# Early part of a decoder block: groups of 1, 1, 2, 2, 2, 4, 4 chunks of w_in, and the norm of x by tokens

## The chip, the cores and the metric

The kernel runs on one core of a Trainium2 chip. The metric is the time of one launch in microseconds (us) as the device reports it; lower is better. One execution of each kernel is taken by the hardware profiler, and its span runs from the first to the last instruction. The engines are TensorE (PE, with its weight loads as PEld), VectorE (DVE), ScalarE (ACT), GpSimd (POOL) and SyncE (SP), which issues most transfers.

## The reference

A decoder block on one sequence of 256 tokens, width 2048, all in fp32. Only its beginning matters here:

```python
c_act = jax.nn.silu(c)
mod = (c_act @ w_ada[l] + b_ada[l])[:, None, :]
sh1, sc1, gt1, sh2, sc2, gt2 = jnp.split(mod, 6, axis=-1)
h = rms_norm(x, g_pre_mix[l]) * (1.0 + sc1) + sh1
z = h @ w_in[l]
...
# two attention branches on z, gates, w_o; then the same with sh2, sc2 and a ConvFFN (w_up, w_down)
```

w_ada is 2048 x 12288 and w_in 2048 x 8000, so both are read once from HBM and used for one vector and 256 tokens.

## The kernel before

Channels lie on the partitions: x is held as xT, 16 chunks of 128 channels by 256 tokens. A product of fp32 numbers is made of three products of rounded ones. Each weight tile of 128 x 1024 (512 KB) is loaded into a buffer raw, ACT casts it to whi (L116), DVE makes wlo as the difference (L117), and PE multiplies whi by h, whi by the low part of h, and wlo by h (mm3, L129 to L131; mm3t, L144 to L146, with the sides swapped). Of raw, whi and wlo there are five buffers each (NW1).

The early part computes a first share of z: 39 blocks of 128 columns of w_in, which end in 20 pairs (tiles of 128 x 512 in SBUF). It runs over groups of chunks of the inner dimension (KGS = 2, 2, 2, 2, 4, 4), so that it can begin before all of w_ada's two first parts (sh1 and sc1) is there. For each group, early_gen makes h of the group's chunks: xT times rstd (L264), the adaLN product of c with the group's columns of w_ada (ada_gen), its result turned onto the partitions by a small matmul (L270), the columns s1 and sh1 (L275 to L277), x times s1 plus sh1 (L282), and the split of h into high and low (split_pair, L158 and L159). Then early_z runs the 39 blocks over the group's chunks; in the first group an ACT copy makes the pairs (L368), in later ones DVE adds to them (L375), or ACT copies and POOL adds for every third pair (L372, L373). The products of one pair end in one of three PSUM banks ("mm").

ada_gen loads tiles of 512 KB into raw2 (four buffers, L102); for the first group every other one goes to raw instead (L95, spread). A chunk takes four such tiles. In each, PE multiplies cpad (silu of c, one column of 32) by the four column groups of the tile (L234). From the fourth group on every second tile is multiplied on DVE instead (SHARE, L240 and L242) and summed by four matmuls (L247).

Ahead of all this x's norm: ACT squares xT by two chunks (L211, two buffers), PE sums over the partitions with a matrix of ones (L213), ACT takes the root (L215) and DVE the reciprocal (L216), all with tokens in the free dimension.

A generator (bg) interleaves the next group's early_gen with the present group's early_z in the program; then a scheduler, which models the engines' times, fixes the order of the instructions on each engine. Each engine works through its own order and waits for semaphores; SP does the same with the transfers. Behind the early part, the matmul that begins the band bias (L328) and the latents' norms (lat) stand in the last group's hooks.

Of the kernel before, what the change touches and what calls it, by code (L numbers as in the profile page):

```python
# [20 lines left out]
NF = DFF // P  # L21
EPS = 1e-6
NEG = -1e30
KGS = [2, 2, 2, 2, 4, 4]
SHARE = [99, 99, 99, 2, 2, 2]
NEARLY = 8
LATS = (3, 4, 5, 6, 7, 8, 9)
HOOKS = (3, 9, 15)
# [10 lines left out]
WT = 1024  # L39
# [4 lines left out]
def block_kernel(ctx: ExitStack, tc: tile.TileContext, a, out: bass.AP):  # L44
    nc = tc.nc
    pe, act, dve, pool = nc.tensor, nc.scalar, nc.vector, nc.gpsimd
    PS = bass.MemoryType.PSUM

    const = ctx.enter_context(tc.tile_pool(name="const", bufs=1))
    dram = ctx.enter_context(tc.tile_pool(name="dram", bufs=1, space=bass.MemoryType.DRAM))  # L50
    hp_ctx = ExitStack()
    hp = hp_ctx.enter_context(tc.tile_pool(name="hp", bufs=8, side="right"))
# [5 lines left out]
    def bank(tag):  # L58
        return psp.tile([P, 512], F32, tag=tag, bufs=PSN[tag], name="bk_" + tag)
# [88 lines left out]
    def turn_pe(o, x):  # L148

        pe.transpose(o, x, ident)  # L150

    split_ins = []

    def split_pair(src, pl, tag, bufs, eng=dve):

        hl = pl.tile([P, 2, 2, T], F32R, tag=tag, bufs=bufs // 2, name=tag)
        src = src.rearrange("p (j t) -> p j t", j=2)
        i0 = act.copy(hl[:, :, 0], src)  # L158
        i1 = eng.tensor_tensor(hl[:, :, 1], src, hl[:, :, 0].bitcast(F32), op=ALU.subtract)  # L159
        split_ins[:] = [i0, i1]  # L160
        return [(hl[:, j, 0], hl[:, j, 1], hl[:, j].rearrange("p a t -> p (a t)")) for j in range(2)]


    blk_ctx = ExitStack()
# [11 lines left out]
    xT = xp.tile([P, KC, T], F32, name="xT")  # L176
# [28 lines left out]
    dve.tensor_copy(cpad[:, :, 0:1], csil.rearrange("p (k o) -> p k o", o=1))  # L205


    ps_ss = bank("tp")
    for k in range(0, KC, 2):
        sq = xp.tile([P, 512], F32, tag="sq", bufs=2, name="sq").rearrange("p (a b) -> p a b", a=2)  # L210
        act.activation(sq, xT[:, k:k + 2, :], AF.Square)  # L211
        for i in range(2):
            pe.matmul(ps_ss[:, :T], ones, sq[:, i, :], start=(k + i == 0), stop=(k + i == KC - 1))  # L213
    rstd = xp.tile([P, T], F32, name="rstd")
    act.activation(rstd, ps_ss[:, :T], AF.Sqrt, scale=1.0 / D, bias=epst)  # L215
    dve.reciprocal(rstd, rstd)  # L216
# [36 lines left out]
    s1 = const.tile([P, KC], F32, name="s1")  # L253
    sh1 = const.tile([P, KC], F32, name="sh1")
    hs = [None] * KC

    def early_gen(kg, k0, s):

        w = s * 64
        with ExitStack() as order:  # L260
            if kg:
                order.enter_context(tc.issue_after(split_ins[1].ins))
            for k in range(k0, k0 + s):
                dve.tensor_tensor(xT[:, k, :], xT[:, k, :], rstd, op=ALU.mult)  # L264
        yield from ada_gen(a["w_ada1"][kg], w, rows, 0, "sc", SHARE[kg], kg == 0)

        nb = w // P
        ps = bank("tp")
        for b in range(nb):
            pe.matmul(ps[:, 4 * b:4 * b + 4], rows[:, b * P:(b + 1) * P], ident[:, 0:P:32], start=True, stop=True)  # L270

        pv = ps[:, :4 * nb].rearrange("p (b g) -> p g b", g=4)
        bs = bada[:, KC + k0:KC + k0 + s].rearrange("p (g b) -> p g b", g=2)
# [12 lines left out]
    sh2 = const.tile([P, KC], F32, name="sh2")

# [51 lines left out]
    def early_z(kg, hooks):  # L339
        s, k0 = KGS[kg], k0s[kg]  # L340
        nblk = 2048 // (s * P)
        order = []
        for i in range(NPAIR):
            order += [("kr", 6)] if i == 6 else [("vs", 7), ("vs2", 7)] if i == 7 else [(0, i), (1, i)]
        src = a["w_in1"][kg]
        b = None
        for off in range(0, len(order), nblk):
            n = min(nblk, len(order) - off)
            w = n * P * s
            wt = Weights(src[:, off * P * s:off * P * s + w], w, WT if n == nblk else n * P * (s // 2))  # L350
            for u in range(n):
                what, i = order[off + u]
                if what in (0, "kr", "vs"):
                    b = bank("mm")
                if what == "vs":
                    for half in range(2):
                        for kk in range(s):
                            mm3t(b[:, half * T:half * T + T], wt.cut(kk * n * P + u * P, 2 * P), hs[k0 + kk], half,
                                 kk == 0, kk == s - 1)
                elif what != "vs2":  # L360
                    c0 = T if what == 1 else 0
                    for kk in range(s):
                        mm3(b[:, c0:c0 + T], wt.cut(kk * n * P + u * P), hs[k0 + kk], kk == 0, kk == s - 1)
                if what in (1, "kr", "vs2"):
                    wd = T if i == 6 else 2 * T
                    if kg == 0:
                        pairs[i] = blkp.tile([P, 512], F32, tag="blk", name="pair")
                        act.copy(pairs[i][:, :wd], b[:, :wd])  # L368
                    elif i % PADD == 1:
                        pl = xp if kg < len(KGS) - 1 else at  # L370
                        part = pl.tile([P, 512], F32, tag="sq" if pl is xp else "tmp", bufs=2, name="part")
                        act.copy(part[:, :wd], b[:, :wd])  # L372
                        pool.tensor_tensor(pairs[i][:, :wd], pairs[i][:, :wd], part[:, :wd], op=ALU.add)  # L373
                    else:
# [543 lines left out]
```

## Time and profile before

| | us |
|---|---|
| median of 3 runs | 1507.36 |
| lowest and highest | 1503.29, 1513.49 |
| profiled execution | 1507.02 |
| its span | 1505.2 |
| PE busy in it | 1455.3 (97%) |
| DVE busy in it | 1080.4 (72%) |
| ACT busy in it | 781.5 (52%) |

The span is what the trace shows from the first to the last instruction; 1.8 us of the execution lie around it. A busy share is an average over the whole span: the early part is its first sixth, and its own bound is read from its own stretches.

### The profile page before, as it was taken

Reading aid. Unit: us, or ns where it says so; the run is one execution under the profiler, and the core shown is the slowest. Engines: PE = TensorE matmul, PEld = TensorE weight load, DVE = VectorE, ACT = ScalarE, POOL = GpSimd, SP = SyncE. Lnnn points to the kernel's source line nnn. Section 1 sums busy time; section 2 is a strip of 40 time slices with the busy share of each in tenths; the row PEclk is TensorE's granted clock in tenths of the full one; section 3 lists DMA queues with packets and bytes.
Section 4 is the critical chain, followed back from the end, with each engine's and each line's share of the span. In section 5 each row is a group of like instructions: output and inputs, shape, how many; then the busy total and the mean of one; then the engine's idle time right before and its main releaser. Section 6 shows DMA issues by size and latency. Waiting matters only on the chain.

```text
span 1505.2 us, 24750 instructions
## 1 busy us (share of the span) xinstructions
PE 1455.3 (97%) x9506; PEld 1280.5 (85%) x9506; DVE 1080.4 (72%) x1472; ACT 781.5 (52%) x1253; POOL 294.9 (20%) x207
## 2 busy tenths in 40 slices
PE   7999999789999899999899999999999999999997
PEld 6988899789898899978688888888888888888886
DVE  3579868988787969777788878877767776444443
ACT  4534435545645555766465545655555555434442
POOL 0034315832524535420000000000000000000000
PEclk9999999999999999999999999999999999999999
DMA  9889868588587858658667778765555557555552
GB/s 373 320 309 325 307 234 263 178 266 289 187 295 238 291 186 268 228 201 336 245 207 270 254 258 263 247 209 186 191 188 192 187 193 243 191 196 190 190 193 99
DMA packets 101525, 356.96 MB, mean 237 GB/s; under 512 B 11760, under 2 KB 12208, under 8 KB 100896
## 3 DMA queue, kind: packets, MB, share of 16 engines
q1 hardware_dynamic: 99936, 350.82, 67.9%
q0 software_dynamic: 1472, 4.58, 1.2%
q8 instruction: 74, 1.21, 0.3%
q14 instruction: 43, 0.35, 0.1%
HBM read 351.11 MB, written 4.24 MB: 236 GB/s over the span
## 4 chain that ended last, share of the span: by engine, by line
PE 72%; DMA 12%; DVE 9%; issue 3%; ACT 2%; POOL 1%; DVEq 0%; SPq 0%; ACTq 0%; POOLq 0%
PE bk_mm L136 10%; PE bk_sc L136 7%; DMA raw<-in_w_ada_dram 6%; PE bk_mm L129 6%; PE bk_mm L131 6%; PE bk_mm L130 6%; PE bk_mm L138 5%; PE bk_mm L144 4%; PE bk_mm L146 4%; PE bk_mm L145 4%; DVE wlo L117 3%; PE bk_sc L145 3%; PE bk_sc L144 3%; PE bk_sc L146 3%; PE bk_sc L138 3%
## 5 line engine op out<-in xcount | busy, mean ns | idle before, releaser
L117 DVE TENSOR_TENSOR wlo<-raw,whi 128x1024 fp32r<-128x1024 f32 (+3 forms) x472 | 589.5, 1257 | 278.0 <-ACT whi L116 276.8
L116 ACT CAST whi<-raw 128x1024 fp32r<-128x1024 f32 (+3 forms) x472 | 478.3, 1021 | 487.7 <-DMA raw<-in_w_up_dram 74.6
L129 PE MATMUL bk_mm<-h,whi 128*128 128x256 f32 x976 | 282.6, 290 | 0.1
L130 PE MATMUL bk_mm<-h,whi 128*128 128x256 f32 x976 | 277.8, 285 | 0.0
L131 PE MATMUL bk_mm<-h,wlo 128*128 128x256 f32 x976 | 277.3, 285 | 0.5 <-DVE wlo L117 0.5
L136 PE MATMUL bk_mm<-h,whi 128*128 128x512 f32 x848 | 266.6, 396 | 0.0
L242 DVE SCALAR_TENSOR_TENSOR acc<-raw,csil,acc 128x1024 f32<-128x1024 f32 (+1 forms) x141 | 190.6, 1352 | 45.1 <-DMA raw<-in_w_ada_dram 44.3
L129 PEld LDWEIGHTS bk_mm<-h,whi 128*128 128x128 f32 x976 | 187.7, 193 | 13.6 <-issue 9.1
L138 PEld LDWEIGHTS bk_mm<-h,wlo 128*128 128x128 f32 x848 | 158.9, 188 | 41.1 <-DVE wlo L117 3.9
L130 PEld LDWEIGHTS bk_mm<-h,whi 128*128 128x128 f32 x976 | 187.9, 193 | 0.8 <-issue 0.8
L131 PEld LDWEIGHTS bk_mm<-h,wlo 128*128 128x128 f32 x976 | 187.6, 193 | 0.9 <-DVE wlo L117 0.7
L136 PE MATMUL bk_sc<-h,whi 128*128 128x512 f32 x560 | 177.0, 398 | 0.0
L138 PE MATMUL bk_mm<-h,wlo 128*128 128x256 f32 x848 | 167.5, 279 | 1.5 <-DVE wlo L117 1.5
L136 PEld LDWEIGHTS bk_mm<-h,whi 128*128 128x128 f32 x848 | 129.2, 189 | 0.5 <-issue 0.4
L138 PEld LDWEIGHTS bk_sc<-h,wlo 128*128 128x128 f32 x560 | 105.3, 189 | 27.5 <-DVE wlo L117 2.8
L762 POOL TENSOR_TENSOR sa<-sa,u 128x512 f32<-128x512 f32 x22 | 33.7, 1531 | 467.8 <-DVE u L756 387.0
L138 PE MATMUL bk_sc<-h,wlo 128*128 128x256 f32 x560 | 110.8, 279 | 1.7 <-DVE wlo L117 1.7
L373 POOL TENSOR_TENSOR pair<-pair,part 128x512 f32<-128x512 f32 x35 | 63.4, 1812 | 192.3 <-ACT part L372 192.2
L136 PEld LDWEIGHTS bk_sc<-h,whi 128*128 128x128 f32 x560 | 85.8, 190 | 0.4 <-ACT whi L116 0.4
L144 PE MATMUL bk_sc<-whi,g 128*128 128x512 f32 x176 | 68.7, 390 | 0.0
L144 PE MATMUL bk_mm<-whi,g 128*128 128x512 f32 x176 | 68.7, 390 | 0.0
L145 PE MATMUL bk_mm<-wlo,g 128*128 128x512 f32 x176 | 68.5, 389 | 0.0
(205 smaller groups left out, 2317.6 us busy)
## 6 DMA issues: line engine op xcount, KB each, us to landing
raw<-in_w_ada_dram SPq DMA_DIRECT2D x192, 512.0 KB, 5.1
raw<-in_w_up_dram SPq DMA_DIRECT2D x176, 512.0 KB, 4.6
raw<-in_w_in_dram SPq DMA_DIRECT2D x116, 512.0 KB, 5.2
raw<-in_w_down_dram SPq DMA_DIRECT2D x88, 512.0 KB, 4.5
raw<-in_w_o_dram SPq DMA_DIRECT2D x32, 512.0 KB, 5.6
raw<-in_w_uqn_dram SPq DMA_DIRECT2D x16, 384.0 KB, 4.0
bias<-trow POOLq DMA_DIRECT2D x16, 256.0 KB, 4.8
raw<-in_w_ukv_dram SPq DMA_DIRECT2D x16, 256.0 KB, 3.5
```

Source lines behind the costliest of these rows:

```text
L116: act.copy(hi[:, :n], raw[:, :n])
L117: dve.tensor_tensor(lo[:, :n], raw[:, :n], hi[:, :n].bitcast(F32), op=ALU.subtract)
L129: pe.matmul(o, wh, xh, start=start, stop=False)
L130: pe.matmul(o, wh, xl, start=False, stop=False)
L131: pe.matmul(o, wl, xh, start=False, stop=stop)
L136: pe.matmul(o, w[0], x[2], start=start and i == 0, stop=False)
L138: pe.matmul(o[:, :T], w[1], x[0], start=False, stop=stop and i == 1)
L144: pe.matmul(o, ch, wh, start=start, stop=False)
L145: pe.matmul(o, ch, wl, start=False, stop=False)
L146: pe.matmul(o, cl, wh, start=False, stop=stop)
L242: dve.scalar_tensor_tensor(acc[:, :w], r, csil[:, j:j + 1], acc[:, :w], op0=ALU.mult, op1=ALU.add)
L373: pool.tensor_tensor(pairs[i][:, :wd], pairs[i][:, :wd], part[:, :wd], op=ALU.add)
```

## The change

The groups become 1, 1, 2, 2, 2, 4, 4 chunks; the products on DVE begin with the fifth group, which is the same chunk as before. A group of one chunk has 64 columns in each of the four column groups of the adaLN product, so a small matmul has 64 columns instead of 128, and two matmuls (L287) turn the result. split_pair can split a single chunk; two single chunks share one buffer. The first adaLN product no longer spreads its tiles over two pools. The norm's sums are taken with the squares as the stationary operand and one column of ones as the moving one, so that the tokens end on the partitions: 32 matmuls (L223) into two banks, a root of two columns (L226), a reciprocal of 128 x 2, and two transposes that bring the result back to the free dimension (L230, in turn_pe), copied by ACT (L232). A root of a constant (L216) is taken ahead of the squares.

```diff
-KGS = [2, 2, 2, 2, 4, 4]
-SHARE = [99, 99, 99, 2, 2, 2]
+KGS = [1, 1, 2, 2, 2, 4, 4]
+SHARE = [99, 99, 99, 99, 2, 2, 2]
...
-    ps_ss = bank("tp")
+    warm = const.tile([P, 1], F32, name="warm")
+    act.activation(warm, epst, AF.Sqrt, scale=0.0, bias=epst)
+    ps_ss = [bank("tp"), bank("o")]
     for k in range(0, KC, 2):
         sq = xp.tile([P, 512], F32, tag="sq", bufs=2, name="sq").rearrange("p (a b) -> p a b", a=2)
         act.activation(sq, xT[:, k:k + 2, :], AF.Square)
         for i in range(2):
-            pe.matmul(ps_ss[:, :T], ones, sq[:, i, :], start=(k + i == 0), stop=(k + i == KC - 1))
+            for t in range(2):
+                pe.matmul(ps_ss[t][:, 0:1], sq[:, i, t * P:t * P + P], ones[:, 0:1], start=(k + i == 0), stop=(k + i == KC - 1))
+    rt = const.tile([P, 2], F32, name="rt")
+    for t in range(2):
+        act.activation(rt[:, t:t + 1], ps_ss[t][:, 0:1], AF.Sqrt, scale=1.0 / D, bias=epst)
+    dve.reciprocal(rt, rt)
+    ps_r = bank("tp")
+    for t in range(2):
+        turn_pe(ps_r[:, t * P:t * P + P], rt[:, t:t + 1].broadcast_to([P, P]))
     rstd = xp.tile([P, T], F32, name="rstd")
-    act.activation(rstd, ps_ss[:, :T], AF.Sqrt, scale=1.0 / D, bias=epst)
-    dve.reciprocal(rstd, rstd)
+    act.copy(rstd, ps_r[:, :T])
...
-        yield from ada_gen(a["w_ada1"][kg], w, rows, 0, "sc", SHARE[kg], kg == 0)
+        yield from ada_gen(a["w_ada1"][kg], w, rows, 0, "sc", SHARE[kg])
...
+        if s == 1:
+            for u in range(2):
+                pe.matmul(ps[64 * u:64 * u + 64, 0:2], rows[:, 0:64], ident[:, 32 * u:P:64], start=True, stop=True)
+            nb, ng = 1, 2
...
-            hs[k:k + 2] = split_pair(xT[:, k:k + 2, :].rearrange("p a b -> p (a b)"), hp, "h", 16)
+            hs[k:k + len(ks)] = split_pair(xT[:, k:k + len(ks), :].rearrange("p a b -> p (a b)"), hp, "h", 16, n=len(ks),
+                                           room=hroom)
...
-            wt = Weights(src[:, off * P * s:off * P * s + w], w, WT if n == nblk else n * P * (s // 2))
+            wt = Weights(src[:, off * P * s:off * P * s + w], w, WT if n == nblk or s == 1 else n * P * (s // 2))
```

The scheduler lays the early part out anew. On SP, at the start of the program, before (w_ada1_0 and w_in1_0 are the first group's tiles, w_ada1_1 the second group's adaLN tiles):

```order
L178 DMA xT_80<-in_xT_dram 128x1024 x4
L102 DMA raw2_155<-in_w_ada1_0_dram 128x1024
L95 DMA raw_165<-in_w_ada1_0_dram 128x1024
L102 DMA raw2_175<-in_w_ada1_0_dram 128x1024
L95 DMA raw_185<-in_w_ada1_0_dram 128x1024
L102 DMA raw2_195<-in_w_ada1_0_dram 128x1024
L95 DMA raw_205<-in_w_ada1_0_dram 128x1024
L102 DMA raw2_215<-in_w_ada1_0_dram 128x1024
L95 DMA raw_225<-in_w_ada1_0_dram 128x1024
L95 DMA raw_246<-in_w_in1_0_dram 128x1024
L102 DMA raw2_255<-in_w_ada1_1_dram 128x1024
L95 DMA raw_265<-in_w_in1_0_dram 128x1024
```

and now, from the last but one adaLN tile of the first group on (x's four and two more stand ahead):

```order
L102 DMA raw2_215<-in_w_ada1_0_dram 128x1024
L102 DMA raw2_233<-in_w_ada1_0_dram 128x1024
L95 DMA raw_262<-in_w_in1_0_dram 128x1024
L95 DMA raw_288<-in_w_in1_0_dram 128x1024
L95 DMA raw_385<-in_w_in1_0_dram 128x1024
L95 DMA raw_409<-in_w_in1_0_dram 128x1024
L95 DMA raw_505<-in_w_in1_0_dram 128x896
L102 DMA raw2_270<-in_w_ada1_1_dram 128x1024
L102 DMA raw2_294<-in_w_ada1_1_dram 128x1024
L102 DMA raw2_391<-in_w_ada1_1_dram 128x1024
L102 DMA raw2_415<-in_w_ada1_1_dram 128x1024
```

The first group's w_in tiles, which alternated with the second group's adaLN tiles, now all stand ahead of them. On PE, around the first product on w_in (L129), before:

```order
L234 MATMUL bk_sc_154<-raw_225,cpad_105 32x128 x8
L270 MATMUL bk_tp_236<-c_ident_85,rows_144 128x4
L234 MATMUL bk_sc_254<-raw2_255,cpad_105 32x128 x8
L129 MATMUL bk_mm_281<-h_243,whi_248 128x256
L129 MATMUL bk_mm_296<-h_243,whi_248 128x256
```

and now:

```order
L150 MATMUL bk_tp_164<-c_ident_85,rt_160 128x128 x2
L250 MATMUL bk_sc_178<-raw2_233,cpad_105 32x64 x6
L250 MATMUL bk_sc_269<-raw2_270,cpad_105 32x64 x16
L250 MATMUL bk_sc_269<-raw2_294,cpad_105 32x64 x3
L287 MATMUL bk_tp_252<-c_ident_85,rows_169 64x2 x2
L250 MATMUL bk_sc_269<-raw2_294,cpad_105 32x64 x13
L250 MATMUL bk_sc_269<-raw2_391,cpad_105 32x64 x16
L250 MATMUL bk_sc_269<-raw2_415,cpad_105 32x64 x2
L129 MATMUL bk_mm_312<-h_259,whi_264 128x256
L129 MATMUL bk_mm_321<-h_259,whi_264 128x256
```

Fifty of the 64 small matmuls of the second group's adaLN product now stand ahead of the first product on w_in, where eight of 64 stood. On ACT, from the last squares to the first h, before:

```order
L211 ACTIVATE sq_137<-xT_80 128x512
L215 ACT_TABLE_LOAD
L215 ACTIVATE rstd_141<-bk_tp_108,epst_89 128x256
L249 COPY rows_144<-bk_sc_154 128x128
L116 CAST whi_248<-raw_246 128x1024
L158 CAST h_243<-xT_80 128x2x256
```

and now:

```order
L220 ACTIVATE sq_148<-xT_80 128x512
L116 CAST whi_264<-raw_262 128x1024
L220 ACTIVATE sq_154<-xT_80 128x512
L116 CAST whi_290<-raw_288 128x1024
L116 CAST whi_387<-raw_385 128x1024
L116 CAST whi_411<-raw_409 128x1024
L226 ACTIVATE rt_160<-bk_tp_110,epst_89 128x1
L226 ACTIVATE rt_160<-bk_o_111,epst_89 128x1
L116 CAST whi_507<-raw_505 128x896
L232 COPY rstd_167<-bk_tp_164 128x256
L265 COPY rows_169<-bk_sc_178 128x64
L165 CAST h_259<-xT_80 128x256
```

The five casts of the first group's w_in tiles, one of which stood ahead of the first h, now all do, four of them ahead of the root of the norm.

## Rows read from the trace of the kernel before

**Rows 1.** The page's busy time of each engine (share of the span, instructions), and the chain that ended last, by engine.

```profile
PE 1455.3 (97%) x9506; PEld 1280.5 (85%) x9506; DVE 1080.4 (72%) x1472; ACT 781.5 (52%) x1253; POOL 294.9 (20%) x207
...
PE 72%; DMA 12%; DVE 9%; issue 3%; ACT 2%; POOL 1%; DVEq 0%; SPq 0%; ACTq 0%; POOLq 0%
```

**Rows 2.** The table by stretches: us, then busy time and instructions of PE, PEld, DVE, ACT and POOL, the granted clock of PE, the busy share of the DMA engines, GB/s.

```profile
0.00:10.00 10.00, 3.92 (x10) 3.21 (x11) 1.02 (x4) 3.35 (x6) 2.13 (x9) 1.00 0.79 277
10.00:20.00 10.00, 9.34 (x136) 6.64 (x134) 1.30 (x1) 4.83 (x7) 0.00 (x0) 1.00 1.02 409
...
30.00:40.00 10.00, 10.00 (x115) 9.01 (x114) 4.60 (x4) 7.21 (x11) 0.00 (x0) 1.00 1.03 407
...
200.00:220.00 20.00, 20.00 (x178) 18.74 (x177) 13.82 (x21) 6.86 (x11) 3.32 (x2) 1.00 0.59 203
...
260.00:280.00 20.00, 19.12 (x150) 18.21 (x149) 20.00 (x15) 14.12 (x18) 19.62 (x10) 1.00 0.64 198
280.00:300.00 20.00, 13.99 (x96) 13.37 (x96) 16.41 (x15) 8.16 (x13) 16.40 (x13) 0.83 0.52 164
```

**Rows 3.** The same table by 2 us around the first product on w_in; the granted clock is the last but two.

```profile
23.00:25.00 2.00, 1.63 (x19) 1.25 (x20) 1.68 (x2) 0.66 (x2) 0.00 (x0) 0.63 1.03 412
25.00:27.00 2.00, 2.00 (x12) 2.00 (x11) 1.96 (x4) 0.67 (x1) 0.00 (x0) 0.51 1.03 410
27.00:29.00 2.00, 2.00 (x28) 1.67 (x28) 0.73 (x1) 1.05 (x1) 0.00 (x0) 1.00 1.03 410
```

**Rows 4.** The timeline of PE up to the first product on w_in: start, us, engine, line, operation, out<-in, count of records (an fp32 matmul has two), and in brackets the idle time before and what ended it.

```profile
6.08 6.61 PE L213 MATMUL bk_tp<-sq,ones 128*128 128x256 f32 x20 [6.08 <-ACT sq L211]
...
20.06 0.65 PE L234 MATMUL bk_sc<-raw,cpad 128*32 128x128 f32 x16 [0.62 <-DMA raw<-in_w_ada_dram]
21.09 0.39 PE L270 MATMUL bk_tp<-c_ident,rows 128*128 128x4 f32 x2 [0.38 <-ACT rows L249]
23.37 0.98 PE L234 MATMUL bk_sc<-raw,cpad 128*32 128x128 f32 x16 [1.90 <-DMA raw<-in_w_ada_dram]
24.27 1.01 PE L129 MATMUL bk_mm<-h,whi 128*128 128x256 f32 x3
```

**Rows 5.** The timeline of ACT, same columns.

```profile
5.30 1.15 ACT L211 ACTIVATE sq<-xT 128x512 f32<-128x512 f32 x2 [2.67 <-DMA xT<-in_xT_dram]
...
16.90 1.28 ACT L215 ACT_TABLE_LOAD   x1 [1.85 <-PE bk_tp L213]
18.19 0.47 ACT L215 ACTIVATE rstd<-bk_tp,epst 128x256 f32<-128x256 f32 x1
20.77 0.27 ACT L249 COPY rows<-bk_sc 128x128 f32<-128x128 f32 x1 [2.10 <-PE bk_sc L234]
21.32 1.05 ACT L116 CAST whi<-raw 128x1024 fp32r<-128x1024 f32 x1 [0.29 <-DMA raw<-in_w_in_dram]
...
24.63 1.04 ACT L116 CAST whi<-raw 128x1024 fp32r<-128x1024 f32 x1 [1.34 <-DMA raw<-in_w_in_dram]
27.19 1.05 ACT L116 CAST whi<-raw 128x1024 fp32r<-128x1024 f32 x1 [1.51 <-DMA raw<-in_w_in_dram]
29.14 0.59 ACT L368 COPY pair<-bk_mm 128x512 f32<-128x512 f32 x1 [0.91 <-PE bk_mm L131]
```

**Rows 6.** The timeline of DVE, same columns.

```profile
18.70 1.75 DVE L216 RECIPROCAL rstd<-rstd 128x256 f32<-128x256 f32 x1 [15.43 <-ACT rstd L215]
20.48 0.76 DVE L264 TENSOR_TENSOR xT<-xT,rstd 128x256 f32<-128x256 f32 x2
...
23.93 1.22 DVE L117 TENSOR_TENSOR wlo<-raw,whi 128x1024 fp32r<-128x1024 f32 x1
...
63.31 0.69 DVE L375 TENSOR_TENSOR pair<-pair,bk_mm 128x512 f32<-128x512 f32 x1 [0.55 <-PE bk_mm L131]
```

**Rows 7.** The timeline of POOL, same columns: two of the additions to a pair.

```profile
65.42 1.28 POOL L373 TENSOR_TENSOR pair<-pair,part 128x512 f32<-128x512 f32 x1 [62.23 <-ACT part L372]
...
94.18 3.91 POOL L373 TENSOR_TENSOR pair<-pair,part 128x512 f32<-128x512 f32 x1 [4.89 <-ACT part L372]
```

**Rows 8.** The timelines of PE and its weight loads further on: L129 before and behind a piece of two small matmuls (four records) and one of eight, the weight loads of two small matmuls on rows (L270), and the band bias's matmul.

```profile
65.63 0.28 PE L129 MATMUL bk_mm<-h,whi 128*128 128x256 f32 x1
...
66.42 0.38 PE L129 MATMUL bk_mm<-h,whi 128*128 128x256 f32 x1
...
66.88 0.28 PE L129 MATMUL bk_mm<-h,whi 128*128 128x256 f32 x1
...
75.82 0.28 PE L129 MATMUL bk_mm<-h,whi 128*128 128x256 f32 x1
...
77.30 0.28 PE L129 MATMUL bk_mm<-h,whi 128*128 128x256 f32 x1
...
158.93 0.53 PEld L270 LDWEIGHTS bk_tp<-c_ident,rows 128*128 128x128 f32 x4
...
240.97 0.83 PE L328 MATMUL bk_tp<-oh,c_rel_bias 32*32 32x384 f32 x2
```

**Rows 9.** The waits of PE between 24 and 420 us, the two longest in total: for whom, us in total, times, the longest.

```profile
PE bk_mm L131 <- DVE wlo L117: 5.4, 3, 4.3
PE bk_sc L544 <- DVE mx L549: 4.9, 2, 2.9
```

More of the change, by code (lines that the diff above doesn't have):

```diff
@@ L152, in block_kernel, with split_pair @@
     split_ins = []
-    def split_pair(src, pl, tag, bufs, eng=dve):
-        hl = pl.tile([P, 2, 2, T], F32R, tag=tag, bufs=bufs // 2, name=tag)
-        src = src.rearrange("p (j t) -> p j t", j=2)
+    def split_pair(src, pl, tag, bufs, eng=dve, n=2, room=None):
+        if room:
+            hl = room.pop()
+        else:
+            hl = pl.tile([P, 2, 2, T], F32R, tag=tag, bufs=bufs // 2, name=tag)
+            if n == 1:
+                room.append(hl[:, 1:])
+        hl = hl[:, :n]
+        src = src.rearrange("p (j t) -> p j t", j=n)
         i0 = act.copy(hl[:, :, 0], src)
@@ L160, in split_pair @@
         split_ins[:] = [i0, i1]
-        return [(hl[:, j, 0], hl[:, j, 1], hl[:, j].rearrange("p a t -> p (a t)")) for j in range(2)]
+        return [(hl[:, j, 0], hl[:, j, 1], hl[:, j].rearrange("p a t -> p (a t)")) for j in range(n)]
     blk_ctx = ExitStack()
@@ L264, in early_gen @@
                 dve.tensor_tensor(xT[:, k, :], xT[:, k, :], rstd, op=ALU.mult)
-        yield from ada_gen(a["w_ada1"][kg], w, rows, 0, "sc", SHARE[kg], kg == 0)
+        yield from ada_gen(a["w_ada1"][kg], w, rows, 0, "sc", SHARE[kg])
         nb = w // P
         ps = bank("tp")
[L269 to L273, printed above, removed]
@@ L274, in early_gen @@
-        s1v = s1[:, k0:k0 + s].rearrange("p (g b) -> p g b", g=2)
-        dve.scalar_tensor_tensor(s1v, pv[:, 0:2, :], 1.0, bs, op0=ALU.add, op1=ALU.add)
+        if s == 1:
+            for u in range(2):
+                pe.matmul(ps[64 * u:64 * u + 64, 0:2], rows[:, 0:64], ident[:, 32 * u:P:64], start=True, stop=True)
+            nb, ng = 1, 2
+        else:
+            ng = 4
+            for b in range(nb):
+                pe.matmul(ps[:, 4 * b:4 * b + 4], rows[:, b * P:(b + 1) * P], ident[:, 0:P:32], start=True, stop=True)
@@ L276, in early_gen @@
+        pv = ps[:, :ng * nb].rearrange("p (b g) -> p g b", g=ng)
+        h = ng // 2
+        bs = bada[:, KC + k0:KC + k0 + s].rearrange("p (g b) -> p g b", g=h)
+        s1v = s1[:, k0:k0 + s].rearrange("p (g b) -> p g b", g=h)
+        dve.scalar_tensor_tensor(s1v, pv[:, 0:h, :], 1.0, bs, op0=ALU.add, op1=ALU.add)
         dve.tensor_tensor(s1[:, k0:k0 + s], s1[:, k0:k0 + s], gcol[:, G_MIX + k0:G_MIX + k0 + s], op=ALU.mult)
-        dve.tensor_tensor(sh1[:, k0:k0 + s].rearrange("p (g b) -> p g b", g=2), pv[:, 2:4, :],
-                          bada[:, k0:k0 + s].rearrange("p (g b) -> p g b", g=2), op=ALU.add)
+        dve.tensor_tensor(sh1[:, k0:k0 + s].rearrange("p (g b) -> p g b", g=h), pv[:, h:ng, :],
+                          bada[:, k0:k0 + s].rearrange("p (g b) -> p g b", g=h), op=ALU.add)
@@ L279, in early_gen @@
         for k in range(k0, k0 + s, 2):
-            for kk in (k, k + 1):
+            ks = [kk for kk in (k, k + 1) if kk < k0 + s]
+            for kk in ks:
                 ht = xT[:, kk, :]
                 dve.tensor_scalar(ht, ht, s1[:, kk:kk + 1], sh1[:, kk:kk + 1], op0=ALU.mult, op1=ALU.add)
-            hs[k:k + 2] = split_pair(xT[:, k:k + 2, :].rearrange("p a b -> p (a b)"), hp, "h", 16)
+            hs[k:k + len(ks)] = split_pair(xT[:, k:k + len(ks), :].rearrange("p a b -> p (a b)"), hp, "h", 16, n=len(ks),
+                                           room=hroom)
@@ L285, in block_kernel @@
+    hroom = []
     s2 = const.tile([P, KC], F32, name="s2")
@@ L590, in step @@
         pool.tensor_tensor(mixs[h // 2][:, e * T:e * T + T], tm[:, 0:T], tm[:, T:512], op=ALU.add)
-    warm = const.tile([P, 1], F32, name="warm")
     bg["gen"] = [cols_gen(0, gt1, 2 * KC, G_PMIX), cols_gen(2, s2, 4 * KC, G_FFN), cols_gen(1, sh2, 3 * KC, None)]
```

## The prediction

> **What bounds the kernel now.** I read the busy shares first: TensorE (PE) is busy 97% of the span, and the chain that ended last is 72% PE [rows 1]. A share of the whole span says little about an edit that touches the first 250 us, so next came the table by stages [rows 2]. From 30 us on PE is busy in every slice up to about 260 us, while VectorE (DVE) has idle time in the same slices; in 260 to 300 us PE idles 7 us. The waits of PE between 24 and 420 us are a few us on DVE [rows 9]; the same question for 24 to 250 us returns no line, so all of them lie behind 250. So up to 250 us time is the start of the first real product plus PE's work, and nothing else can be won there.
>
> The start is read from the timelines. PE's first product of the first weights stands at 24.27 us [rows 4]. Two chains end just before it. The norm: squares, sums on PE, a table load of 1.28, a root of 0.47, a reciprocal of 1.75 that ends at 20.45 [rows 5, 6]. The adaLN product: its last transfer releases PE at 20.06, the copy of it starts at 20.77, one small matmul follows at 21.09 [rows 4, 5]. They are even. Behind both stand the transfers, 409 GB/s from 10 us on with a busy share of 1.02 [rows 2]. They are used in the order in which SP issues them: x's four are 1 to 4, the eight of the first adaLN product are 5 to 12, then w_in and the next adaLN product alternate. Transfer 1 releases ACT at 5.30, 12 PE at 20.06, 13 ACT at 21.32, 14 PE at 23.37, 15 ACT at 24.63, 17 ACT at 27.19 [rows 4, 5]: (27.19 - 5.30) / 16 = 1.37 us a transfer. The first product of before thus stood behind the 14th transfer, which PE handles at 23.37, straight ahead of it.
>
> **The change, part by part.** *The start.* A single chunk needs four adaLN transfers, not eight: numbers 5 to 8, in at 5.30 + 7 x 1.37 = 14.9 us. But the order of SP then has all five w_in transfers (9 to 13) and only after them the four of the second chunk (14 to 17). PE's order puts all but 14 of the 64 matmuls of that second product, two of the fourth transfer among them, ahead of the first L129. PE works in order, so the first product now waits for transfer 17, not 14. That transfer number came at 27.19 in before; the fifth w_in transfer is 7/8 as large (-0.17): **27.0 us, 2.7 later**. The new wait's queue is all of PE. No order of landing makes it shorter than the bytes: 17 transfers less an eighth, with the small tables, are 9.0 MB, and the trace has moved 2.77 MB by 10 us and 409 GB/s after [rows 2], so 25.3 us at the least (+1.0).
>
> The Trainium skill, "DMA: Bandwidth & Descriptors", section "Queues, rings and completion order", says that completion is not first-in first-out per issuing engine, since 16 engines finish on their own. By that the sum could fall to the +1.0 of the bytes; the releases above keep the order of issue, so the trace gives it no weight here.
>
> *The norm with tokens on the partitions.* Sixteen matmuls of 256 columns go, 32 of one column come, each with its own load of 128x128 weights. Nearest rows: two matmuls of four columns with four weight loads take 0.53 [rows 8], so about 0.23 each at full clock, 7.4 for 32, against 6.61 for the first ten of before [rows 4]. At half clock it is twice that. The table load moves ahead of x's first transfer at 5.30 and costs nothing; the reciprocal of 128x2 and the broadcast by two transposes replace 1.75 by under 1. None of this sets the end, because ACT's order now has the casts of w_in (L116) in front of it: the last square stands behind the cast of transfer 9, and the root (L226) behind the casts of 10 to 12. Transfer 12 lands at 5.30 + 11 x 1.37 = 20.4, its cast ends at 21.4, two roots end by 22.4, the transposes by 23.0, the copy of rstd behind one more cast by 23.6, x times rstd (0.38) by 24.0. The small matmul on rows (L287) stands on PE behind transfer 15 (24.5); then the two columns, x times s, and the cast of h take some 1.3: 26.0. Transfer 17 at 27.0 is later by 1.0, so a cold PE that makes the sums 1 us slower costs nothing, and one 3 us slower costs 2.
>
> *PE's work behind the start.* The matmuls on w_in are 1500 up to the band bias's matmul (L328, at 240.97 [rows 8]) in both orders. Between them stand 48 pieces with 235 small matmuls before, 46 with 259 now. A piece of two matmuls costs 1.25 - 0.72 = 0.53 of PE's time (L129 at 65.63, 66.42, 66.88, where three steps of 0.12 are its usual pace); one of eight costs 1.48 - 0.72 = 0.76 [rows 8]. So 0.45 a piece and 0.04 a matmul: -0.9 + 1.0 = **0.1**, nothing. (The sum closes: 1500 x 0.12 + 48 x 0.45 + 235 x 0.04, with some 2 for wider ones and 2 for the slow clock at the start, is 215 of the 216.7 us between the two rows.)
>
> *The twenty extra sums.* One group more means 20 more additions to the pairs: 13 on DVE at 0.69 and 7 by an ACT copy of 0.59 and a POOL addition of 1.28 [rows 5 to 7]. They fall into the second group, at about 50 to 70 us. That group lasts 117 x 0.12 = 14 plus eight adaLN pieces at 0.76, about 20 us; DVE needs 9 for the sums, 6 for five splits and 3 for x: 18. In the first group ACT copies 20 pairs in 11.8, casts five times in 5.2 and has 1 of small work, 18 against PE's 14 + 6 + 1 for the clock. Both fit, and three banks let PE run ahead; were the adaLN pieces not there, ACT's surplus would be 18 - 14 = 4. One of these pieces needs transfer 26, in at 39.5, where PE comes by at 39.1. I take **0.4** for all such waits, bounds 0 and 4.
>
> *The clock.* Granted clock is 0.63 and 0.51 from 23 to 27 us, after a PE with little to do, and full from 27 on [rows 3]: the low level, 1.2 GHz. Now PE is idle for longer ahead of the start; the products then run as slowly as before at first. I take 0, bounds -1 and +2.
>
> Sum: 2.7 + 0.1 + 0.4 + 0 = 3.2. The profiled execution took 1507.0 (span 1505.2 and 1.8 around it), its median of three is 1507.4; the orders behind the early part are the same but for a few swapped neighbours. **1507 + 3 = 1510 us.**
>
> **The rivals.** *The delay is swallowed.* In 260 to 300 us PE idles 7 us on DVE and POOL [rows 2, 9]; if they had work queued from earlier, a PE 3 us late would lose nothing: 1507. For it speaks that DVE is full in that stretch; against it, that DVE has 6 us idle in 200 to 220, so it brings no backlog along and follows PE.
>
> *It does what its words say.* If the first product started from the first chunk, transfer 8 at 14.9 plus the 4.2 us from 20.06 to 24.27 gives 19.1, 5.2 earlier: 1502. This decides only if transfers 14 to 17 are in by then; at 1.37 each they are not.
>
> *POOL becomes the bound of the second group.* Its seven sums pass through two buffers, and ACT, in order, waits for them with the weight casts behind it. The rows have 1.28 and 3.91 for the same addition [rows 7]. It decides from 20 / 7 = 2.9 us a sum; at 3.91 the group takes 27.4, 7 more: 1507 + 3 + 7 = 1517, slower.
>
> **How the numbers follow.** Chances: forecast 0.62, swallowed 0.2, its words 0.08, POOL 0.1. Three runs of before span 1503.3 to 1513.5, so a median may sit 3 to 4 off. From 1507 less 4 to POOL's 1517: the range is 1503 to 1517, which leaves out the case of 1502 and some of the noise. One per cent, 15 us, is about what a measurement of this kernel can tell from no change. No single case reaches it: faster by more would need three times the second rival (0.02), slower by more POOL with the full 4 of ACT and a late norm (0.04), the rest is within it (0.94).
>
> **What would show it.** The first L129 at about 27.0 us, released by a transfer of w_ada, with small matmuls of the second chunk around it; the root (L226) not before 21; the band bias's matmul (now L354) at about 244; no PE wait between 30 and 240 over 1 us; the same gaps from 250 on, 3 us later. I am wrong if L129 starts before 25.3, if PE shows waits on ACT's copies or on POOL's sums in 30 to 70 us, or if that matmul's shift is gone at 420.

## The result and the profile after

The changed kernel takes 1523.86 us (median of four runs, 1520.55 to 1525.04) against 1508.28 for the kernel before beside it: a ratio of 1.0106, 95% interval 1.0086 to 1.0126. It is 15.6 us slower, where 3 were forecast, and lies outside the range. The profiled execution took 1525.04 us (span 1522.9, so 17.7 more than before).

The page after, where before has [rows 1]: PE's share is the same, and the chain that ended last says nothing of the cause.

```profile
PE 1471.2 (97%) x9674; PEld 1290.8 (85%) x9674; DVE 1099.0 (72%) x1489; ACT 786.3 (52%) x1265; POOL 295.0 (19%) x214
...
PE 70%; DVE 12%; DMA 11%; issue 4%; ACT 2%; POOL 0%; DVEq 0%; SPq 0%; ACTq 0%; POOLq 0%
```

So the shift is followed along the program by events that both traces have. The first product on w_in (L129) stands at 30.79 instead of 24.27 [rows 4]: +6.5. The band bias's matmul (now L354), the end of the early part, is at 249.91 instead of 240.97 [rows 8]: +8.9. It stays at +8 to +10 up to 692 us, is +11 at 1250, and +17.7 at the end. By stretches: 6.5 up to the first product, 2.4 from there to the band bias, 1.9 up to the first matmul of w_down, 6.9 from that to its last one (241.0 us in before, 247.9 after). The 1.9 can't be read as an effect: over the traces of all kernels here that stretch takes 1010.6 to 1022.3 us. Two stretches thus lose time for sure: the start, and the last part, in which nothing was changed.

The start, in PE's timeline after (columns as in [rows 4]):

```profile
6.57 0.56 PE L223 MATMUL bk_tp<-ones,sq 128*128 128x1 f32 x2 [6.57 <-ACT sq L220]
6.99 0.56 PE L223 MATMUL bk_o<-ones,sq 128*128 128x1 f32 x2
7.42 0.57 PE L223 MATMUL bk_tp<-ones,sq 128*128 128x1 f32 x2
...
22.89 0.56 PE L223 MATMUL bk_o<-ones,sq 128*128 128x1 f32 x2
23.38 1.49 PE L250 MATMUL bk_sc<-raw,cpad 128*32 128x64 f32 x44
...
26.87 0.28 PE L287 MATMUL bk_tp<-c_ident,rows 128*64 128x2 f32 x4
27.08 1.37 PE L250 MATMUL bk_sc<-raw,cpad 128*32 128x64 f32 x58
30.43 0.43 PE L250 MATMUL bk_sc<-raw,cpad 128*32 128x64 f32 x4 [1.98 <-DMA raw<-in_w_ada_dram]
30.79 1.01 PE L129 MATMUL bk_mm<-h,whi 128*128 128x256 f32 x3
```

A one-column matmul of the norm takes 0.43 us (6.57, 6.99, 7.42), 32 take 13.7, and the last ends at 23.4. The adaLN matmuls (L250) stand among them in PE's order and release raw2's buffers only as they come by. SP, whose order has the adaLN transfers behind, waits for that: us in total, times, the longest, in the first 31 us. (In before the same kind of wait is 4.3 us for L102 and 2.1 for L95, without a gap in the transfers.)

```profile
SPq L102 <- PE bk_sc L250: 12.9, 6, 4.4
```

And the transfers, which in before ran at 1.02 and 409 GB/s from 10 us on [rows 2], run dry. Columns as in [rows 2, 3]:

```profile
10.00:20.00 10.00, 10.00 (x88) 9.44 (x88) 0.00 (x0) 4.87 (x7) 0.00 (x0) 1.00 1.03 420
...
24.00:26.00 2.00, 2.00 (x58) 1.50 (x51) 0.06 (x1) 0.95 (x2) 0.00 (x0) 1.00 0.38 98
...
30.00:32.00 2.00, 1.57 (x13) 1.10 (x13) 2.00 (x4) 0.00 (x0) 0.00 (x0) 0.50 0.95 324
...
34.00:36.00 2.00, 2.00 (x11) 2.00 (x11) 0.78 (x1) 0.85 (x2) 0.00 (x0) 0.50 1.00 408
36.00:38.00 2.00, 2.00 (x32) 1.58 (x31) 0.00 (x0) 1.02 (x3) 0.00 (x0) 0.79 1.03 418
```

The last rows also show the products at the low level of the clock from 30 to over 36 us; before it was 23 to 27 [rows 3]. PE's waits between 24 and 250 us, none in before behind the start:

```profile
PE bk_mm L129 <- DVE pair L401: 2.1, 5, 0.6
PE bk_sc L250 <- DMA raw<-in_w_ada_dram: 2.0, 1, 2.0
PE bk_mm L129 <- ACT part L398: 0.2, 1, 0.2
```

The second stretch is w_down (L144 to L146, 128x512), in the same order in both kernels and without a wait. The costliest groups of PE in before and then in after (busy, mean ns of one):

```profile
L144 PE MATMUL bk_mm<-whi,g 128*128 128x512 f32 x176 | 68.7, 390 | 0.0
```

```profile
L144 PE MATMUL bk_mm<-whi,g 128*128 128x512 f32 x176 | 69.8, 396 | 0.0
```

All six groups of w_down, 1056 matmuls, moved from 389 or 390 ns to 395 or 396; their busy time together is 6.6 us longer. What differs is the place of the operands. rt (L224), 8 bytes a partition, is a new tile, and by the sides of the tile pools in the kernel what lies behind it on its side of SBUF moves (raw, whi, wlo, xT, g among them; for g and whi the 32 bytes stand in c_pad32's expectation); what lies on the other side (h, a second set of whi and wlo) doesn't.

### The profile page after: what moved, and what is told of

It is laid out like the page before. It is cut to its first block, busy times and chain, and to the rows that moved or that the text cites. A ratio compares the mean times of both kernels' runs of the same rounds, so it can differ in the third digit from the quotient of the medians.

```text
span 1522.9 us, 25133 instructions
## 1 busy us (share of the span) xinstructions
PE 1471.2 (97%) x9674; PEld 1290.8 (85%) x9674; DVE 1099.0 (72%) x1489; ACT 786.3 (52%) x1265; POOL 295.0 (19%) x214
## 4 chain that ended last, share of the span: by engine, by line
PE 70%; DVE 12%; DMA 11%; issue 4%; ACT 2%; POOL 0%; DVEq 0%; SPq 0%; ACTq 0%; POOLq 0%
PE bk_mm L136 8%; DMA raw<-in_w_ada_dram 7%; PE bk_mm L129 6%; PE bk_mm L131 6%; PE bk_mm L130 6%; PE bk_sc L136 5%; DVE wlo L117 5%; PE bk_mm L144 4%; PE bk_mm L145 4%; PE bk_mm L146 4%; PE bk_mm L138 4%; DVE acc L258 4%; PE bk_sc L145 3%; PE bk_sc L144 3%; PE bk_sc L146 3%
## 5 line engine op out<-in xcount | busy, mean ns | idle before, releaser
L117 DVE TENSOR_TENSOR wlo<-raw,whi 128x1024 fp32r<-128x1024 f32 (+2 forms) x472 | 599.5, 1278 | 268.1 <-ACT whi L116 267.3
L116 ACT CAST whi<-raw 128x1024 fp32r<-128x1024 f32 (+2 forms) x472 | 477.7, 1020 | 486.3 <-PE bk_sc L146 72.1
L129 PE MATMUL bk_mm<-h,whi 128*128 128x256 f32 x976 | 283.2, 291 | 2.3 <-DVE pair L401 2.1
L130 PE MATMUL bk_mm<-h,whi 128*128 128x256 f32 x976 | 277.5, 285 | 0.0
L258 DVE SCALAR_TENSOR_TENSOR acc<-raw,csil,acc 128x1024 f32<-128x1024 f32 (+1 forms) x141 | 194.6, 1380 | 47.6 <-DMA raw<-in_w_ada_dram 47.1
L129 PEld LDWEIGHTS bk_mm<-h,whi 128*128 128x128 f32 x976 | 186.8, 192 | 16.4 <-issue 9.3
L130 PEld LDWEIGHTS bk_mm<-h,whi 128*128 128x128 f32 x976 | 186.6, 191 | 0.4 <-issue 0.3
L399 POOL TENSOR_TENSOR pair<-pair,part 128x512 f32<-128x512 f32 x42 | 67.6, 1609 | 198.5 <-ACT part L398 198.3
L144 PE MATMUL bk_sc<-whi,g 128*128 128x512 f32 x176 | 69.8, 396 | 0.0
L144 PE MATMUL bk_mm<-whi,g 128*128 128x512 f32 x176 | 69.8, 396 | 0.0
L146 PE MATMUL bk_sc<-whi,g 128*128 128x512 f32 x176 | 69.6, 396 | 0.0
```

The lines of the kernel that those rows point to most:

```text
L116: act.copy(hi[:, :n], raw[:, :n])
L117: dve.tensor_tensor(lo[:, :n], raw[:, :n], hi[:, :n].bitcast(F32), op=ALU.subtract)
L129: pe.matmul(o, wh, xh, start=start, stop=False)
L130: pe.matmul(o, wh, xl, start=False, stop=False)
L144: pe.matmul(o, ch, wh, start=start, stop=False)
L146: pe.matmul(o, cl, wh, start=False, stop=stop)
```

## The experiments

Theories: **place** (the 32 bytes cost some 5 us late in the program), **norm** (the one-column sums cost the start), **groups** (the groups themselves). Their rivals stand in the expectations. Times are medians; ratios are against before on the same chip, in brackets the 95% interval.

### Each part alone, on one chip

```diff
     # c_pad32: before, plus one tile
+    const.tile([P, 2], F32, name="pad")
     # d_unshift: after, rt without a tile of its own
-    rt = const.tile([P, 2], F32, name="rt")
+    rt = cth[:, 0:2]
```

```diff
     # a_groups: after, with the norm of before (shown: the sums)
-                pe.matmul(ps_ss[t][:, 0:1], sq[:, i, t * P:t * P + P], ones[:, 0:1], start=(k + i == 0), stop=(k + i == KC - 1))
+            pe.matmul(ps_ss[:, :T], ones, sq[:, i, :], start=(k + i == 0), stop=(k + i == KC - 1))
     # b_norm: d_unshift, with the groups of before
-KGS = [1, 1, 2, 2, 2, 4, 4]
+KGS = [2, 2, 2, 2, 4, 4]
```

Both leave rt's tile out as well; w_down's row reads 390 ns in both, as in before.

> The kernel before with one more tile of 8 bytes per partition (32 with rounding) ahead of rows, and nothing else: every order of instructions stays as it was, only what lies behind it in SBUF from the left moves by 32 bytes, as in the changed kernel (g from 25312 to 25344, the first part's whi from 45792 to 45824). Theory 'place in SBUF': the pitch of PE's products goes with the place, so w_down's goes from 0.227 to 0.234 us a matmul as in the changed kernel (+6.8 us over its 1056 products), w_o's +1.6, and the early part's from 0.121 to 0.118 (-4.6): 1510 to 1514 in all, with the first product on w_in still at 24.3. Rival 'execution': PE was a little slower in that one execution, for any kernel: 1508 and a pitch of 0.227.

> The changed kernel with its two-column root kept in cth, so that the tiles behind stand where they stood in the kernel before; orders as in the changed kernel. 'Place in SBUF': w_down's pitch back at 0.227, the early part's back at 0.121, the first product still at 30.8, total 1518 to 1521. 'Execution': 1524 with a pitch that has nothing to do with the place.

> The groups alone: the norm and its root as before, places in SBUF as before. The scheduler now puts the first product on w_in straight behind the first chunk's four transfers, ahead of the second chunk's product. Theory 'the norm's matmuls of one column delay the start': the sums end at 17 again, the first product at 19 to 21 us, total 1503 to 1507. Rival 'the cut itself costs' (twenty more sums and the second group's transfers behind the first group's): first product early, but the gain is lost to waits of PE between 30 and 70 us: 1508 to 1514.

> The norm by tokens alone: groups of 2, 2, 2, 2, 4, 4 and the places in SBUF as before. 'The norm's matmuls delay the start': 32 matmuls at 0.43 end at 21 to 23 us instead of 17, the first product at 28 to 31 instead of 24.3, total 1512 to 1516. Rival 'hidden': the eight transfers of the first adaLN product end at 20 in any case, so the start moves by under 2 us: 1508 to 1510.

| kernel | us | ratio | first L129 | band bias |
|---|---|---|---|---|
| c_pad32 | 1513.82 | 1.0027 [1.0015, 1.0040] | 23.87 | 238.82 |
| d_unshift | 1519.15 | 1.0066 [1.0043, 1.0089] | 31.38 | 250.84 |
| a_groups | 1512.69 | 1.0026 [1.0013, 1.0039] | 22.04 | 246.90 |
| b_norm | 1515.18 | 1.0047 [1.0032, 1.0063] | 31.58 | 248.37 |

An unused tile makes before slower. Taking rt's tile away brings after from 1.0106 to 1.0066, though the two intervals just touch; w_down's row is the firmer evidence, and goes with the place, in c_pad32 and then in d_unshift:

```profile
L144 PE MATMUL bk_mm<-whi,g 128*128 128x512 f32 x176 | 69.8, 396 | 0.0
```

```profile
L144 PE MATMUL bk_mm<-whi,g 128*128 128x512 f32 x176 | 68.6, 390 | 0.0
```

Taken apart step by step, the 1.06% is 0.40 place (after to d_unshift), 0.40 norm (d_unshift to a_groups) and 0.26 groups (a_groups to before), about 6, 6 and 4 us (after was timed apart from the others, each ratio against before beside it). Each alone on top of before gives 0.27 (c_pad32), 0.47 (b_norm) and 0.26 (a_groups), 1.00 together. b_norm alone has the late start with the old groups too: the norm makes it. The last sums on PE, before and then b_norm, and what the first product of b_norm waits for:

```profile
15.69 1.13 PE L213 MATMUL bk_tp<-sq,ones 128*128 128x256 f32 x4
```

```profile
23.61 0.56 PE L216 MATMUL bk_o<-ones,sq 128*128 128x1 f32 x2
...
31.58 0.62 PE L129 MATMUL bk_mm<-h,whi 128*128 128x256 f32 x3 [0.80 <-ACT h L158]
```

The sums end some 7 us later than in before, and so does the start, which here waits for h and not for a transfer.

The groups' own 4 us were a surprise, since a_groups starts 2.2 us sooner than before and yet reaches the band bias 5.9 later. PE's waits in a_groups between 24 and 250 us, and its timeline at the end of the second group:

```profile
PE bk_mm L129 <- ACT h L165: 1.5, 1, 1.5
PE bk_mm L129 <- DVE pair L392: 0.7, 2, 0.4
PE bk_mm L130 <- DVE h L166: 0.5, 1, 0.5
PE bk_mm L131 <- DVE wlo L117: 0.3, 1, 0.3
```

```profile
63.37 0.64 PE L241 MATMUL bk_sc<-raw,cpad 128*32 128x128 f32 x16
65.51 0.61 PE L129 MATMUL bk_mm<-h,whi 128*128 128x256 f32 x3 [1.50 <-ACT h L165]
66.60 0.39 PE L130 MATMUL bk_mm<-h,whi 128*128 128x256 f32 x1 [0.47 <-DVE h L166]
```

The group of one chunk is too short for the eight adaLN transfers of the next: their last piece is at 63.4, h comes after it, PE waits, and the clock is 0.50 at 68 to 70. From the first product to the band bias a_groups takes 224.9 us, before 216.7. Of the 8.2, 8.0 are worked out, not tested: waits 3.0; the low clock on 3.4 + 3.3 us instead of 2.7, half of it lost, 2.0; and five adaLN transfers that PE handled ahead of the start in before and now handles among products, 5 x 0.6 = 3.0. By this, what starts sooner has that much more left to do.

### What the sums cost

```diff
 # e_half: d_unshift; DVE adds the two chunks of squares first
+        dve.tensor_tensor(sq[:, 0, :], sq[:, 0, :], sq[:, 1, :], op=ALU.add)
-        for i in range(2):
-            for t in range(2):
-                pe.matmul(ps_ss[t][:, 0:1], sq[:, i, t * P:t * P + P], ones[:, 0:1], start=(k + i == 0), stop=(k + i == KC - 1))
+        for t in range(2):
+            pe.matmul(ps_ss[t][:, 0:1], sq[:, 0, t * P:t * P + P], ones[:, 0:1], start=(k == 0), stop=(k == KC - 2))
```

> The changed kernel with rt in cth (the addresses of before, as d_unshift, 1519.2 us) and DVE adding the two chunks of squares ahead of the sums, so that 16 one-column matmuls remain of 32. The scheduler then puts only four adaLN transfers ahead of the first product on w_in, as in a_groups. Theory sums: the 32 matmuls at 0.43 us, 13.7 in all, are what d_unshift loses against a_groups (1512.7, the old sums): the first product at 21 to 23 us instead of 31.4, 1512 to 1514 us. Rival: the other new pieces of the norm (two transposes, the copy of rstd behind casts, the root behind casts) cost it: the first product at 24 or later, 1516 us or more.

1514.93 us, 1.0043 [1.0026, 1.0059]; the first product at 22.80, as the sums theory has it, the time 1 us above its band. The start came 8.6 us sooner than in d_unshift, the band bias only 3.0 (247.87 against 250.84): the rest, by the same reckoning, is the work that no longer lies ahead of the start. The run doesn't part the sums from the order: with half of them the scheduler put only four adaLN transfers ahead of the first product, as in a_groups, where after has 50 of the second chunk's 64 small matmuls there too.

```diff
 # m_forms: d_unshift; the matmul by pairs of chunks (lo: weights, rhs: moving, w: columns written)
+                if k == 2:
+                    st, w, rhs = dict(start=True, stop=True), (8, 12), ones[:, 0:4]
+                elif k == 4:
+                    st, w = dict(start=True, stop=True), (8, 9)
+                elif k == 6:
+                    lo = sq[:, t, i * P:i * P + P]
+                    o = i
+                elif k == 8:
+                    st, w, rhs, lo = dict(start=True, stop=True), (128, 256), sq[:, i, t * P:t * P + P], ones
+                elif k == 10:
+                    st, w, rhs, lo = dict(start=True, stop=True), (8, 9), sq[:, i, t * P:t * P + 1], ones
```

> d_unshift with the forms of the sums changed by pairs of chunks, to price one matmul of each; the norm leaves out the sums of chunks 2 to 5 and 8 to 11, whose matmuls write a bank that nobody reads. Chunks 0, 1 and 12 to 15 as they are; 2, 3 with four columns moving and no accumulation; 4, 5 one column, no accumulation; 6, 7 twice in a row into the same bank; 8, 9 the ones as weights and 128 columns of squares moving; 10, 11 the ones as weights and one column moving. Theory weights: each fp32 load of 128x128 weights costs 0.43 us when nothing longer runs beside it, so all forms take 0.43. Rival accumulation: the sums in one place wait for each other: 2 to 5 take 0.23 as the small matmuls on rows do. Rival fresh weights: only weights that have just been changed cost it, those with ones as weights take 0.23 or less.

PE's timeline of m_forms, then the granted clock (the last but two) in two stretches of it:

```profile
6.12 0.56 PE L236 MATMUL bk_tp<-ones,sq 128*128 128x1 f32 x2 [6.12 <-ACT sq L221]
6.54 0.57 PE L236 MATMUL bk_o<-ones,sq 128*128 128x1 f32 x2
...
7.82 3.55 PE L236 MATMUL bk_mm<-ones,sq 128*128 128x4 f32 x16
11.23 0.99 PE L236 MATMUL bk_tp<-ones,sq 128*128 128x1 f32 x4
...
13.79 2.08 PE L236 MATMUL bk_mm<-sq,ones 128*128 128x128 f32 x8
...
17.81 0.38 PE L236 MATMUL bk_tp<-ones,sq 128*128 128x1 f32 x2
18.06 0.36 PE L236 MATMUL bk_o<-ones,sq 128*128 128x1 f32 x2
18.28 0.36 PE L236 MATMUL bk_tp<-ones,sq 128*128 128x1 f32 x2
...
19.71 0.54 PE L236 MATMUL bk_tp<-ones,sq 128*128 128x1 f32 x2
20.11 0.56 PE L236 MATMUL bk_o<-ones,sq 128*128 128x1 f32 x2
```

```profile
17.80:18.70 0.90, 0.90 (x10) 1.00 0.99 396
...
19.70:20.50 0.80, 0.80 (x6) 0.54 1.01 389
```

All three theories fall. The eight matmuls of chunks 2 to 5 (16 records from 7.82 to 11.23) take 0.43 each without accumulation, with four columns or one, and twice into one bank is the same (11.23 to 12.09). The forms with the ones as weights came as the clock rose and can't be compared. But the unchanged form, fresh weights and all, costs 0.43 at 6 us, 0.22 at 18, behind the wide matmuls of 13.79, and over 0.40 from 19.7 on, where the clock's column falls to 0.54. The price goes with the clock: 0.22 at 2.4 GHz, 0.43 at 1.2. From 6 to 12 us PE ran at the low level, though the column reads 1.00 there.

### Raising the clock ahead of the sums

```diff
 # f_warm: d_unshift; ps_w is a bank that nobody reads
+    for _ in range(5):
+        pe.matmul(ps_w[:, :T], ones, ones[:, 0:1].broadcast_to([P, T]), start=True, stop=True)
...
         act.activation(sq, xT[:, k:k + 2, :], AF.Square)
+        pe.matmul(ps_w[:, :T], ones, sq[:, 1, :], start=True, stop=True)
```

> d_unshift (1519.2 us, first product on w_in at 31.4) with 13 matmuls more, all 256 columns wide and into a bank that nobody reads: five ahead of x's sums and one for each pair of chunks. Theory clock: ahead of the start PE runs at its low level whatever the granted clock's column reads there (m_forms: the same one-column matmul took 0.43 us from 6 to 11 and 0.22 from 17.8 to 19.7, behind wide ones), and wide matmuls raise it. Then the 32 sums take 0.22 each, 7 us, plus 8 wide ones at 0.43, 3.4: 10.5 where there were 13.7, the small adaLN matmuls take half, the first product stands at 26 to 28 and its clock is up: 1512 to 1516 us. Rival: the one-column sums keep 0.43 or the bytes set the start: the added 3.4 to 5 us come on top, the first product at 31 or later, 1519 to 1524 us.

1521.42 us, 1.0091 [1.0062, 1.0119]: the time is the rival's, the reason each theory's in part. PE's timeline, and the table by stretches (all engines, columns as in [rows 2]):

```profile
2.24 4.63 PE L220 MATMUL bk_mm<-ones 128*128 128x256 f32 x10 [2.24 <-POOL epst L191]
...
7.52 0.36 PE L227 MATMUL bk_tp<-ones,sq 128*128 128x1 f32 x2
7.74 0.36 PE L227 MATMUL bk_o<-ones,sq 128*128 128x1 f32 x2
...
13.22 0.57 PE L227 MATMUL bk_o<-ones,sq 128*128 128x1 f32 x2
13.65 0.56 PE L227 MATMUL bk_tp<-ones,sq 128*128 128x1 f32 x2
...
34.60 0.71 PE L129 MATMUL bk_mm<-h,whi 128*128 128x256 f32 x3
```

```profile
8.00:10.00 2.00, 2.00 (x16) 1.95 (x17) 0.00 (x0) 0.66 (x2) 0.00 (x0) 1.00 1.03 416
10.00:12.00 2.00, 2.00 (x31) 1.76 (x30) 0.00 (x0) 1.23 (x2) 0.00 (x0) 0.77 1.02 410
12.00:14.00 2.00, 2.00 (x8) 1.82 (x8) 0.00 (x0) 0.00 (x0) 0.00 (x0) 0.50 1.03 412
```

Behind the wide matmuls the first twelve sums take 0.22 (7.52 to 7.74), as the clock theory says. But the clock falls at about 11 us, behind mostly one-column matmuls, with PE busy in every slice and a wide matmul for each pair of chunks; the other twenty sums take 0.43. They end at 27.4, the added work comes on top, and the start moves to 34.60.

```diff
 # a_warm: a_groups
+    for _ in range(6):
+        pe.matmul(ps_w[:, :T], ones, ones[:, 0:1].broadcast_to([P, T]), start=True, stop=True)
```

> The groups of the change with the old norm (a_groups, 1512.7 us, first product at 22.04, a low clock until 26) with six wide matmuls on ones ahead of x's sums, into a bank that nobody reads. Theory clock: the sums of 256 columns, about 0.8 us each in the first us, take 0.43 from the first on, the root comes some 3 us sooner, the first product at 19 to 20: 1509 to 1511 us. Rival: the start is set by the transfers, or what starts sooner waits at the end of the groups: 1512 to 1514.

1515.25 us, 1.0051 [1.0032, 1.0069]: neither theory's range; it wasn't faster than a_groups. Its trace was taken from its slowest execution, 1522.07, and shows the order, not the price. The scheduler set another order: behind the third pair of sums PE waits 2.0 us for an adaLN transfer (to 11.36), the squares wait for their buffers, five casts instead of two stand ahead of the first h on ACT, and the first product is at 25.75.

### The place again

```diff
     # c_pad64: before, plus a tile of 64 bytes (c_pad128: [P, 32])
+    const.tile([P, 16], F32, name="pad")
     # g_rt64: after
-    rt = const.tile([P, 2], F32, name="rt")
+    rt = const.tile([P, 16], F32, name="rt")[:, 0:2]
```

> Before with an unused tile of 64 bytes ahead of rows, where c_pad32 had one of 32: every tile behind it on the left of SBUF moves by 64 bytes, the orders stay those of before. Theory parity: what counts is where a tile stands within a step of 64 bytes (c_pad32 moved that, 64 doesn't): 1508 us, 128x512 matmuls of w_down every 0.227 us, early ones every 0.1214. Rival drift: any place but the old one is slower, by 5 us for 32 bytes: 1514 or more, w_down 0.234 or more.

> The same with 128 bytes. Theory parity: as before, 1508 us and 0.227 us in w_down. Rival drift: 1514 us or more. A third way, a pattern of 128 or 256 bytes, would show as a third value of the pitch in this run or in the one with 64 bytes.

> The changed kernel once more, beside the next three on the same chip: 1522 to 1525 us by all theories.

> The changed kernel with rt as a tile of 64 bytes a partition instead of 8 (which takes 32): the orders are those of the changed kernel, the tiles behind it stand 64 bytes from their places of before, not 32. Theory place: 64 bytes cost little (c_pad64, +1), so the time is that of d_unshift, 1519 to 1520, and the matmuls of w_down take about 0.227 us. Rival: the place has nothing to do with the last 5 us, c_pad32's 4 us were something else: 1523 to 1524, w_down at 0.234.

| kernel | us | ratio | mean ns, w_down L144 | band bias |
|---|---|---|---|---|
| c_pad64 | 1511.58 | 1.0008 [0.9993, 1.0023] | 395 | 236.97 |
| c_pad128 | 1512.03 | 1.0026 [1.0009, 1.0043] | 395 | 241.11 |
| after_2 | 1522.89 | 1.0097 [1.0075, 1.0119] | 396 | 252.23 |
| g_rt64 | 1517.80 | 1.0069 [1.0042, 1.0096] | 395 | 248.46 |

A larger rt gives 5.1 us back with the same orders, but this doesn't confirm the theory: its intervals overlap with after_2's, w_down's pace, which was to come back, didn't, and of the 5.3 us between the two traces 2.8 lie ahead of the first product (33.55 in after_2, 30.79 in g_rt64 and in after itself). Parity falls too: w_down is slow in all four. What does stand is the pace of w_down. From its first to its last matmul it takes 241.0 us in each of the eight traces with the old places, 247.9 in each of the five with 32 or 64 bytes more, and 247.1 in c_pad128. What 64 bytes win is elsewhere, in the early products. The group of L130 in c_pad32 and then in c_pad64:

```profile
L130 PE MATMUL bk_mm<-h,whi 128*128 128x256 f32 x976 | 277.0, 284 | 0.0
```

```profile
L130 PE MATMUL bk_mm<-h,whi 128*128 128x256 f32 x976 | 273.4, 281 | 0.0
```

c_pad64 is at the band bias 4.0 us ahead of before and gives it back in w_down. g_rt64 has 281 there as well, after_2 284. Which addresses make which product fast stays open. No version beat before.

## Why the prediction was wrong

**The price of the one-column sums failed first.** The text had both values, 0.23 at full clock and twice that at half, and built on the full one; the column of the granted clock does read 1.00 ahead of the start. Measured: 0.43, 13.7 us for the 32 and not 7.4. Before's own trace held a sign of it: of the 20 records of its first ten sums [rows 4], five lie in 6 to 8 us and ten in 10 to 12, under a column of 1.00 in both. In the traces' clock records the first entry, the rise to full speed, comes at 9.9 us in before, 16.3 in m_forms and 26.6 in after; ahead of it nothing is recorded, and the column shows 1.00. The Trainium skill, "TensorE: Matmul & The Clock Gate", section "What's actually happening", says that the low level is the default and activity releases it; m_forms and f_warm agree at the start: 0.43 first, 0.22 behind wide matmuls. In f_warm the clock was then at 0.50 with PE 2.00 of 2.00 us busy (12 to 14 us), so the level can't be read off a row's busy share.

**"None of this sets the end" failed with it.** The text allowed 2 us for sums that end 3 us late, along the chain to h. It missed the other chain: adaLN matmuls stand among the sums, hold raw2's buffers, and SP stops. "1.37 us a transfer" took an unbroken stream for granted. This chain is read from the trace of after; no run tests it by itself. That the first product waits for an adaLN transfer of the second chunk, with that chunk's small matmuls around it, was right (released at 30.43); the transfer came 3.4 us later than the 27.0. The start cost 6.5 where 2.7 was put.

**Clock 0** was low: 30.79 to 36.8 (the column's 0.79 in the last row) instead of 24.27 to 27 at half speed costs (6.0 - 2.7) / 2, some 1.7, within the text's bounds of -1 and 2. **The extra sums**, 0.4 within 0 to 4, measured 2.3 of waits, 2.1 of them on DVE and 0.2 on ACT's copies. **PE's work 0.1**: it can't be told apart, since the place makes the early products some 2 us faster (c_pad32: 215.0 us between the two events, before 216.7). Behind the start after takes 2.4 us more than before: 1.7 + 2.3 - 1.7 is 2.3.

**The rivals.** Nothing was swallowed: +8.9 at 250 us, +9.6 at 692. POOL held nobody: PE has no wait on its sums. "Its words" at 19.1 was ruled out for the right reason, but a_groups shows what it would have been worth: a start 2.2 us sooner, and the time given back.

**The place wasn't thought of at all.** Some 5 of the 15.6 us (6.9 in w_down, less what the early products win) are due to it, and w_down lies outside the part of the program that the text looked at, its order unchanged; "the same gaps from 250 on" was wrong there.

## What to carry to other kernels

Price a matmul ahead of the first real products at the low clock, and take the price from rows there, not from the clock's column; in after 32 one-column matmuls cost 13.7 us at the low level with PE busy in every slice. Before adding work to an engine's early order, name whose buffers are released behind it, and which queue waits for these. A new tile, however small, moves others: compare the addresses of two builds, and test an edit without the shift before giving its time to the edit.

## What the runs showed of the hardware

- The granted clock's column reads 1.00 until the first fall in the trace, also while the same one-column fp32 matmul takes 0.43 us, its price at 0.50 (m_forms: 6 to 12 us, and from 19.7).
- That price doesn't depend on one or four columns, accumulation or the bank (m_forms).
- A shift of 32 bytes of operands in SBUF changes the mean of w_down's 128x512 matmuls from 390 to 396 ns; 64 bytes make the early 128x256 ones faster (L130: 285 ns in before, 284 with 32 bytes, 281 with 64) and leave the others slow. The rule behind it isn't known.
